# Encoder step on one core: the first three weight units as one operand of 328 columns

## The chip, the cores and the metric

The kernel runs on one core of one Trainium2 chip. The metric is the device time in microseconds (us) of one execution. The kernel before took 838.03, 839.92 and 839.5 us in three runs, median 839.5 us.

## What is computed

Two layers of a streaming encoder over 320 tokens (256 of a prompt, 64 of a running stream), width 1024. Each layer projects, attends in two branches, and adds two normalised sublayers:

```
h = x @ w_in
A = band attention (8 heads, learned bias by distance)
B = sparse attention (8 heads, rotary); an indexer picks the keys:
    score[t,s] = sum_h w[t,h] * relu(q_idx[t,h] . k_idx[s])
x = LayerNorm(alpha * x + concat(A, B) @ w_out)
x = LayerNorm(alpha * x + relu(x @ w_up)^2 @ w_down)
```

Only the projection of layer 0 and the indexer behind it matter here. The indexer key has 64 columns of `w_in` and the indexer weights 8 more (together `ki`, 72 columns); the indexer queries are four blocks of 128 columns (`qi0` to `qi3`).

## The kernel before

Weights come in **units** of 1024 x 128 (8 row blocks of 128 rows). Layer 0 begins with the units ki (unit 0, 72 columns), qi0, qi3, qi2, qi1 (units 1 to 4), then qa0, qa1, va2, ka0, va1, ka1 and so on (units 5 to 10 and up). Two units lie next to each other in HBM and come as one load of 1024 KB (`load_raw`, L151) into one of two buffers named `raw`; a third load waits until the pair two before it is split. So the loads behind the first three units are the pairs (3,4), (5,6), (7,8), (9,10), (11,12), (13,14).

All products are float32 made of three: a unit is **split** into a rounded high part `wh` (ScalarE, L170) and the rest `wl` (VectorE, L176), and so is x; `mm3` (L188 to L190) then multiplies hi*hi, hi*lo and lo*hi into the same bank. A unit takes 8 x 3 = 24 matmuls of 320 columns. `project` multiplies one unit with all 8 row blocks of x and hands the bank to the unit's use. Four PSUM banks are for these products (`main_acc`), four (`at`) for everything else, so a set of three `at` banks must be emptied before the next set but one can begin.

The uses of the first units, in words:

- ki: ScalarE evacuates the bank (L284), doubles the 64 rows (L492) and swaps halves (`swap`, L292, four instructions); VectorE rotates (`rotate`, L295 to L297), and the finished key is written out (`o_ki`, L499, a DMA on SP).
- qi0 to qi3: evacuate, swap, rotate in the same way. Then a **round of dots** (`Index.dots`, L533 and L535) multiplies the query with the keys into three `at` banks, `clip` (L541, ScalarE, three instructions) empties them, and `weigh` adds them up. After four rounds VectorE begins to pick keys.

No engine chooses its order at run time. The program is written down in the order of a virtual clock: every use is put on an agenda (`later`) with a delay from the table `WAIT`, each `mm3` advances the clock by `NEXT`, and what is due is written into the queues of the engines. `prefetch(i + AHEAD)`, called when a projection begins, writes the splits of the next four units ahead of that. Each queue (ScalarE, VectorE, TensorE, GpSimd and SP, which issues all DMAs) then runs strictly in that order. SP also waits, before each DMA, for the landing of the eighth DMA before it. In SP's queue the write of `o_ki` stands ahead of the bias loads of the first band pair (`u<-rel`, six loads, L341), two cache loads (`kca`, `vca`), and the load of units 11 and 12; then follow the same loads for the next two pairs and the load of units 13 and 14.

At the start, x comes in five loads, ki and qi0 by two row blocks at a time, qi3 in two halves; units 0 and 1 are multiplied together, row block by row block, and unit 2 after them. The split parts of the first three units take three of the five `wh`/`wl` buffers, and units 1 and 2 take one of the two `raw` buffers.

Of the kernel before, what the change touches and what calls it, by code (L numbers as in the profile page):

```python
# [11 lines left out]
F32 = mybir.dt.float32  # L12
F32R = mybir.dt.float32r
AF = mybir.ActivationFunctionType
ALU = mybir.AluOpType

P = 128
DEPTH = 2
D = 1024
KD = D // P  # L20
TP = 256
TS = 64
T = TP + TS
TX = T + 2
# [10 lines left out]
TAKEN = -3.0e38  # L35
BARRED = -1.0e38
N_UNIT = 67
N_DIST = 447
AHEAD = 4
N_DEFER = 7  # L40
N_OUTER = 2
N_SIDE = 4
N_WARM = 7
N_TAIL = 4
TOKENS = slice(0, P), slice(P, 2 * P), slice(T - P, T)
WAIT = [{"lo": 3.4, "rope": 4.6, "scores": 3.4, "peaks": 0.0, "exps": 1.0, "normalise": 5.6, "turn": 3.0,
# [18 lines left out]
NEXT = 3 * 0.136  # L65
# [4 lines left out]
def encoder_step(ctx: ExitStack, tc: tile.TileContext, a: dict):  # L70
    nc = tc.nc
# [11 lines left out]
    def st(shape, tag, bufs, dt=F32):  # L83
        uid[0] += 1
        return sb.tile(shape, dt, name=f"{tag}_{uid[0]}", tag=tag, bufs=bufs)
# [22 lines left out]
    def unit(dt=F32, w=T):  # L108
        return st([P, 3 * P], "u", N_UNIT, dt)[:, :w]

# [28 lines left out]
    raw = {}  # L139
    split = {}  # L140
    at = {"raw": 0, "split": 0}

    def load_raw(i):
        l, c = units[i]
        if c is None:
            t = st([P, 2, KD, P], "raw", 2)
            nc.sync.dma_start(t[:, 0, :, :72], a["w_ki"][l])
            raw[i] = t[:, 0, :, :72]
        elif c % 2 == 0:
            t = st([P, 2, KD, P], "raw", 2)  # L150
            nc.sync.dma_start(t, a["w_all"][l, c // 2])  # L151
            raw[i] = t[:, 0]
            raw[i + 1] = t[:, 1]

    def need_raw(upto):
        while at["raw"] <= min(upto, len(units) - 1):
            load_raw(at["raw"])
            at["raw"] += 1
# [22 lines left out]
    def until(ready):  # L181
        while not ready():
            advance(NEXT)
# [9 lines left out]
    x = ct([P, KD, T], "x")  # L193
# [3 lines left out]
    rope = ct([P, 4, T], "rope")  # L197
    ln = ct([P, DEPTH, 4, KD], "ln")
# [1 line left out]

    nc.gpsimd.memset(mean_w, -1.0 / D)
    xs = [(unit(F32R), unit(F32R)) for _ in range(KD)]
    pair0 = st([P, 2, KD, P], "raw", 2)
    raw[0], raw[1], raw[2] = st([P, KD, TX], "rl", 1)[:, :, :72], pair0[:, 0], pair0[:, 1]
    ins = a["w_ki"][0], a["w_all"][0, 0, :, 0], a["w_all"][0, 0, :, 1]
    for i, n in enumerate((72, P, P)):
        split[i] = [st([P, KD, P], t, 5, F32R)[:, :, :n] for t in ("wh", "wl")]
    at["raw"], at["split"] = 3, 3
    cuts = [slice(0, 1), slice(1, 2)] + [slice(k, k + 2) for k in range(2, KD, 2)]
    for g in cuts:  # L210
        nc.sync.dma_start(x[:, g], a["xT"][:, g])
        if g.start != 1:
            g = slice(g.start - g.start % 2, g.start + 2)
            for i in range(2):
                nc.sync.dma_start(raw[i][:, g], ins[i][:, g])
    for g in (slice(0, 4), slice(4, KD)):
        nc.sync.dma_start(raw[2][:, g], ins[2][:, g])
    need_raw(3)
    make_identity(nc, ident)
    nc.gpsimd.memset(eps, EPS)  # L220
    warm = main_acc()
    for _ in range(N_WARM):
        nc.tensor.matmul(warm[:, :P], mean_w, mean_w, start=True, stop=True)

    def split_rows(i, g):
        hi, lo = split[i]
        nc.scalar.activation(hi[:, g], raw[i][:, g], AF.Copy)  # L227
        nc.vector.tensor_tensor(lo[:, g], raw[i][:, g], hi[:, g].bitcast(F32), op=ALU.subtract)  # L228

    for g in cuts:  # L230
        for k in range(g.start, g.stop):
            nc.scalar.activation(xs[k][0], x[:, k], AF.Copy)
            nc.vector.tensor_tensor(xs[k][1], x[:, k], xs[k][0].bitcast(F32), op=ALU.subtract)  # L233
        if g.start != 1:
            g = slice(g.start - g.start % 2, g.start + 2)
            for i in range(2):
                split_rows(i, g)
    for g in (slice(0, 4), slice(4, KD)):
        split_rows(2, g)
    need_raw(5)  # L240
    nc.sync.dma_start(rope, a["rope"])
    nc.sync.dma_start(ln, a["ln"])
    fresh = set(range(KD))
    whole = {0, 1, 2}
    rh, rl = st([P, KD, TX], "rh", 1, F32R), st([P, KD, TX], "rl", 1, F32R)

    stats = []

    def project(i, defer, *uses):

        prefetch(i + len(uses) - 1 + AHEAD)
        accs = []
        for n in range(len(uses)):
            accs.append(main_acc()[:split[i + n][0].shape[2]])
        for k in range(KD):
            until(lambda: k in (norm.ready if defer else fresh))
            for n, p in enumerate(accs):
                if defer:
                    mm3(p[:, :TX], i + n, k, rh[:, k], rl[:, k], k == 0, k == KD - 1)
                else:  # L260
                    mm3(p[:, :T], i + n, k, *xs[k], k == 0, k == KD - 1)

        def settle(p, use):
            if not stats:
                later(NEXT, settle, p, use)
                return
            n = p.shape[0]
            mu, rstd = stats
            c, u = st([P, 1], "c", 6)[:n], temp("z", 3)[:n]
            nc.vector.scalar_tensor_tensor(u, mu[:n], p[:, T:T + 1], p[:, :T], op0=ALU.mult, op1=ALU.add)  # L270
            nc.vector.tensor_copy(c, p[:, T + 1:TX])
            nc.vector.tensor_tensor(u, u, rstd[:n], op=ALU.mult)  # L272
            later(NEXT, use, (u, c))

        for p, use in zip(accs, uses):
            if defer:
                settle(p, use)
            else:
                use((p[:, :T], None))
# [383 lines left out]
    class LastNorm(Norm):  # L663


        def __init__(self, l, which):
            super().__init__(l, which, False)
            self.rg = st([P, KD, TX], "rh", 1)[:, :, :T]
            self.g_row = st([P, KD, TX], "rl", 1)[0:1, 0:4].rearrange("p k t -> p (k t)")[:, :D]
            nc.sync.dma_start(self.g_row, a["g_last"])  # L670
            self.ones = unit(w=P)
            nc.gpsimd.memset(self.ones, 1.0)
# [76 lines left out]
    for l in range(DEPTH):  # L749
# [25 lines left out]
        for s, (name, j) in enumerate(W_IN_ORDER[l]):  # L775
            br = name[1]
            if name[1] in "ab" and (br, j) not in pairs:
                pairs[br, j] = Pair(l, br, j, bias_tiles(l, j) if br == "a" else index.mask)
            uses.append(partial(take, name, j))
            if l > 0 or s > 0:  # L780
                project(base + s + 1 - len(uses), l > 0 and s < N_DEFER, *uses)
                uses = []

# [5 lines left out]
        accs = [main_acc() for _ in range(N_OUTER)]  # L789
# [5 lines left out]
        for m in range(KD):  # L795
            if m < N_OUTER:
                p = accs[m]
            else:
                prefetch(wo + m + AHEAD)
                p = main_acc()  # L800
# [26 lines left out]
        for m in range(KD):  # L827
            if m % 2 == 0:
                later(2.0, before.apply, m)
            p = main_acc()  # L830
# [10 lines left out]
        if not final:  # L841
            fresh.clear()
            xs = [(unit(F32R), unit(F32R)) for _ in range(KD)]
# [24 lines left out]
def lay_out(i):  # L868
    c = np.ascontiguousarray
    xt = np.concatenate([i["x_prompt"][0], i["x_sample"][0]], 0)  # L870
    out = {"xT": c(xt.T.reshape(KD, P, T).transpose(1, 0, 2)), "rope": rope_tables()}
    w = i["w_in"].reshape(DEPTH, KD, P, -1)
    out["w_ki"] = c(w[:, :, :, KI_AT:KI_AT + 72].transpose(0, 2, 1, 3))

    def blocks(w, starts):
        b = np.stack([w[:, :, :, s:s + P] for s in starts], 1)
        return b.transpose(0, 1, 3, 2, 4)

    starts = [[W_IN_AT[n] + P * j for n, j in order if n != "ki"] for order in W_IN_ORDER]
    parts = [np.concatenate([blocks(w[l:l + 1], starts[l]) for l in range(DEPTH)])]  # L880
    parts.append(blocks(i["w_out"].reshape(DEPTH, KD, P, D), range(0, D, P)))
    parts.append(blocks(i["w_up"].reshape(DEPTH, KD, P, DFF), range(0, DFF, P)))
    wd = i["w_down"].reshape(DEPTH, 4, KD, P, KD, P).transpose(0, 4, 1, 3, 2, 5)
    parts.append(wd.reshape(DEPTH, 32, P, KD, P))
    wa = np.concatenate(parts, 1)
    out["w_all"] = c(wa.reshape(DEPTH, 50, 2, P, KD, P).transpose(0, 1, 3, 2, 4, 5))
    for br in "ab":
        k = i[f"cache_{br}_k"][:, 0]
        out["kc" + br] = c(k.reshape(DEPTH, PAST, NPAIR, P).transpose(0, 2, 3, 1))
        v = i[f"cache_{br}_v"][:, 0]  # L890
        out["vc" + br] = c(v.reshape(DEPTH, 2, P, NPAIR, P).transpose(0, 3, 2, 1, 4))
    ki = i["cache_b_kidx"][:, 0].transpose(0, 2, 1)
    out["kidx"] = c(np.concatenate([ki, ki], 1))
    r = i["rel_bias"]
    out["rel"] = c(np.concatenate([np.repeat(r[:, :, 256:], N_DIST - 256, 2), r[:, :, :0:-1]], 2))
    lns = np.stack([i["ln1_g"], i["ln1_b"], i["ln2_g"], i["ln2_b"]], 1)
    out["g_last"] = c(i["ln2_g"][DEPTH - 1:])
    out["ln"] = c(lns.reshape(DEPTH, 4, KD, P).transpose(3, 0, 1, 2))
    return out
# [33 lines left out]
```

## Time and profile before

| | before |
|---|---|
| median of three runs | 839.5 us (838.03 to 839.92) |
| profiled execution | 836.99 us, span 835.2 us |
| mean granted clock of TensorE | 0.993 of full |
| TensorE matmul busy | 821.1 us, 98% of the span |
| VectorE, ScalarE busy | 594.6 us (71%), 494.0 us (59%) |
| DMA | 124.05 MB, mean 149 GB/s |

The span is what the profile covers; the execution's own time is 1.8 us longer. Busy shares are means over the whole kernel, and the change touches the first stage only, so the rows further down are those of the first 70 us. An "idle before" in square brackets ends with what released the engine.

### The profile page before, as it was taken

Reading aid. Unit: us, or ns where it says so; the run is one execution under the profiler, and the core shown is the slowest. Engines: PE = TensorE matmul, PEld = TensorE weight load, DVE = VectorE, ACT = ScalarE, POOL = GpSimd, SP = SyncE. Lnnn points to the kernel's source line nnn. Section 1 sums busy time; section 2 is a strip of 40 time slices with the busy share of each in tenths; the row PEclk is TensorE's granted clock in tenths of the full one; section 3 lists DMA queues with packets and bytes.
Section 4 is the critical chain, followed back from the end, with each engine's and each line's share of the span. In section 5 each row is a group of like instructions: output and inputs, shape, how many; then the busy total and the mean of one; then the engine's idle time right before and its main releaser. Section 6 shows DMA issues by size and latency. Waiting matters only on the chain.

```text
span 835.2 us, 15008 instructions
## 1 busy us (share of the span) xinstructions
PE 821.1 (98%) x5792; PEld 794.3 (95%) x5792; DVE 594.6 (71%) x1284; ACT 494.0 (59%) x955; POOL 28.7 (3%) x145
## 2 busy tenths in 40 slices
PE   9979999999999999999998999999999999999997
PEld 7969999999999999999998989999999999999995
DVE  5649878586998883545496679996699888545343
ACT  6846798565665553434358977885556655434332
POOL 0110000000000000000000010110000000000000
PEclk9999999999999999999999999999999999999998
DMA  8676343343444444534687324342334444434411
GB/s 275 192 191 180 135 143 126 125 151 103 151 156 147 152 154 149 177 127 155 194 171 261 108 101 135 120 177 74 136 145 151 152 151 152 160 144 152 151 51 64
DMA packets 35033, 124.05 MB, mean 149 GB/s; under 512 B 6033, under 2 KB 21521, under 8 KB 22290
## 3 DMA queue, kind: packets, MB, share of 16 engines
q1 hardware_dynamic: 34962, 123.10, 44.6%
q8 instruction: 46, 0.75, 0.4%
q14 instruction: 25, 0.20, 0.1%
HBM read 116.36 MB, written 6.72 MB: 147 GB/s over the span
## 4 chain that ended last, share of the span: by engine, by line
PE 75%; DVE 10%; ACT 8%; DMA 4%; SPq 1%; issue 1%; ACTq 0%; DVEq 0%
PE mm L188 23%; PE mm L189 23%; PE mm L190 23%; DMA raw<-w_all 4%; DVE wl L176 2%; ACT u L292 2%; ACT wh L170 2%; ACT u L418 1%; DVE u L577 1%; PE at L442 1%; DVE m L575 1%; PE at L394 1%; DVE u L410 1%; PE at L461 1%; PE at L396 1%
## 5 line engine op out<-in xcount | busy, mean ns | idle before, releaser
L188 PE MATMUL mm<-u,wh 128*128 128x320 f32 (+1 forms) x1048 | 328.8, 314 | 0.3 <-ACT wh L227 0.2
L190 PE MATMUL mm<-u,wl 128*128 128x320 f32 (+1 forms) x1048 | 324.0, 309 | 0.4 <-DVE wl L176 0.3
L189 PE MATMUL mm<-u,wh 128*128 128x320 f32 (+1 forms) x1048 | 323.8, 309 | 0.2 <-DVE u L233 0.2
L170 ACT ACTIVATE wh<-raw 128x1024 fp32r<-128x1024 f32 x199 | 209.5, 1055 | 182.9 <-PE mm L189 108.4
L176 DVE TENSOR_TENSOR wl<-raw,wh 128x1024 fp32r<-128x1024 f32 x199 | 241.3, 1217 | 57.8 <-ACT wh L170 57.3
L188 PEld LDWEIGHTS mm<-u,wh 128*128 128x128 f32 (+1 forms) x1048 | 196.8, 188 | 2.1 <-ACT wh L227 1.0
L190 PEld LDWEIGHTS mm<-u,wl 128*128 128x128 f32 (+1 forms) x1048 | 196.5, 187 | 1.6 <-DVE wl L228 0.9
L189 PEld LDWEIGHTS mm<-u,wh 128*128 128x128 f32 (+1 forms) x1048 | 196.9, 188 | 0.4 <-DVE u L233 0.4
L188 PE MATMUL mm<-rh,wh 128*128 128x322 f32 x568 | 177.5, 313 | 0.0
L190 PE MATMUL mm<-rh,wl 128*128 128x322 f32 x568 | 176.2, 310 | 0.0
L189 PE MATMUL mm<-rl,wh 128*128 128x322 f32 x568 | 175.8, 310 | 0.0
L189 PEld LDWEIGHTS mm<-rl,wh 128*128 128x128 f32 x568 | 107.2, 189 | 0.2
L188 PEld LDWEIGHTS mm<-rh,wh 128*128 128x128 f32 x568 | 107.1, 189 | 0.2
L190 PEld LDWEIGHTS mm<-rh,wl 128*128 128x128 f32 x568 | 106.5, 188 | 0.0
L603 DVE SCALAR_TENSOR_TENSOR x<-x,mm 128x320 f32<-128x320 f32 x31 | 15.0, 487 | 78.9 <-PE mm L190 78.9
L292 ACT ACTIVATE u<-u 32x320 f32<-32x320 f32 x104 | 48.7, 469 | 1.8
L270 DVE SCALAR_TENSOR_TENSOR z<-mu,mm 128x320 f32<-128x320 f32 x71 | 38.7, 545 | 12.7 <-PE mm L190 12.7
L811 ACT ACTIVATE z<-z,c 128x320 f32<-128x320 f32 x64 | 35.8, 560 | 16.8 <-DVE z L272 15.8
L418 ACT ACTIVATE u<-u,mx 128x128 f32<-128x128 f32 (+2 forms) x80 | 37.0, 464 | 8.9 <-DVE mx L413 8.9
L605 ACT ACTIVATE rh<-x,ln 128x320 fp32r<-128x320 f32 x24 | 13.5, 563 | 45.4 <-DVE x L603 45.4
L818 DVE TENSOR_TENSOR u<-h,u 128x320 fp32r<-128x320 f32 x64 | 31.5, 492 | 7.2 <-DVE h L817 0.5
L272 DVE TENSOR_TENSOR z<-z,rstd 128x320 f32<-128x320 f32 x71 | 34.9, 492 | 0.0
(135 smaller groups left out, 710.4 us busy)
## 6 DMA issues: line engine op xcount, KB each, us to landing
raw<-w_all SPq DMA_DIRECT2D x99, 1024.0 KB, 4.8
u<-rel SPq DMA_DIRECT2D x16, 128.0 KB, 5.5
u<-rel SPq DMA_DIRECT2D x16, 80.0 KB, 5.8
o_va<-u SPq DMA_DIRECT2D x8, 160.0 KB, 5.3
o_ka<-u SPq DMA_DIRECT2D x8, 160.0 KB, 2.3
o_kb<-u SPq DMA_DIRECT2D x8, 160.0 KB, 1.8
o_vb<-u SPq DMA_DIRECT2D x8, 160.0 KB, 1.8
o_y<-x SPq DMA_DIRECT2D x8, 160.0 KB, 1.9
```

What stands on the lines that cost most here:

```text
L170: nc.scalar.activation(hi, w, AF.Copy)
L176: nc.vector.tensor_tensor(lo, w, hi.bitcast(F32), op=ALU.subtract)
L188: nc.tensor.matmul(out, hi[:, k], xh, start=first, stop=False)
L189: nc.tensor.matmul(out, hi[:, k], xl, start=False, stop=False)
L190: nc.tensor.matmul(out, lo[:, k], xh, start=False, stop=last)
L270: nc.vector.scalar_tensor_tensor(u, mu[:n], p[:, T:T + 1], p[:, :T], op0=ALU.mult, op1=ALU.add)
L272: nc.vector.tensor_tensor(u, u, rstd[:n], op=ALU.mult)
L292: nc.scalar.activation(dst[32 * q:32 * q + 32], src[32 * (q ^ 1):32 * (q ^ 1) + 32], AF.Copy)
L418: nc.scalar.activation(p, p, AF.Exp, bias=self.mx[:, i:i + 1], scale=1.0, accum_out=self.sums[:, i:i + 1])
L603: nc.vector.scalar_tensor_tensor(r, r, ALPHA, psum, op0=ALU.mult, op1=ALU.add)
L811: nc.scalar.activation(u, u, AF.Relu, bias=b)
L818: nc.vector.tensor_tensor(hl, h, hh.bitcast(F32), op=ALU.subtract)
```

## The change

The first three units become one operand of 328 columns (72 + 128 + 128), laid out on the host as `w_first`, row block by row block. It comes in eight loads of 164 KB, one per row block, into general buffers; the first two are issued by ScalarE, the rest by SP between the loads of x. Each row block is split as a whole into the buffers `rh`/`rl`, that are free at this time, so all five `wh`/`wl` buffers and both `raw` buffers stay free. The three units are multiplied in one call of `project`: per row block nine matmuls. The load of units 3 and 4 is cut in two halves. There is one warming matmul less.

```
-N_WARM = 7
+N_FIRST = 3
+FIRST_W = 72 + 2 * P
+N_WARM = 6
...
+            if i == N_FIRST:
+                for n in range(2):
+                    nc.sync.dma_start(t[:, n], a["w_all"][l, c // 2, :, n])
+            else:
+                nc.sync.dma_start(t, a["w_all"][l, c // 2])
...
+    fw = [unit(w=FIRST_W) for _ in range(KD)]
+    fh, fl = st([P, KD, FIRST_W], "rh", 1, F32R), st([P, KD, FIRST_W], "rl", 1, F32R)
+    for i, (c0, c1) in enumerate(((0, 72), (72, 72 + P), (72 + P, FIRST_W))):
+        split[i] = fh[:, :, c0:c1], fl[:, :, c0:c1]
...
+    for k in range(2):
+        nc.scalar.dma_start(fw[k], a["w_first"][:, k])
     for g in cuts:
         nc.sync.dma_start(x[:, g], a["xT"][:, g])
+        for k in range(max(g.start, 2), g.stop):
+            nc.sync.dma_start(fw[k], a["w_first"][:, k])
     need_raw(3)
+    nc.sync.dma_start(rope, a["rope"])
+    need_raw(5)
+    nc.sync.dma_start(ln, a["ln"])
...
+    for k in range(KD):
+        nc.scalar.activation(xs[k][0], x[:, k], AF.Copy)
+        if k == 0:
+            nc.vector.tensor_copy(fh[:, k], fw[k])
+        else:
+            nc.scalar.activation(fh[:, k], fw[k], AF.Copy)
+        nc.vector.tensor_tensor(xs[k][1], x[:, k], xs[k][0].bitcast(F32), op=ALU.subtract)
+        nc.vector.tensor_tensor(fl[:, k], fw[k], fh[:, k].bitcast(F32), op=ALU.subtract)
...
+            if i == 0:
+                for part, of in ((0, 0), (0, 1), (1, 0)):
+                    for n, p in enumerate(accs):
+                        nc.tensor.matmul(p[:, :T], split[n][part][:, k], xs[k][of], start=k == 0 and part + of == 0,
+                                         stop=k == KD - 1 and part == 1)
+                advance(N_FIRST * NEXT)
+                continue
...
-            if l > 0 or s > 0:
+            if l > 0 or s > N_FIRST - 2:
                 project(base + s + 1 - len(uses), l > 0 and s < N_DEFER, *uses)
```

Because `project` now begins with three units, its first call of `prefetch` writes the splits of units 3 to 6 (before: 3 to 5), and the uses of ki, qi0 and qi3 are all due after the same projection. That moves instructions in the queues. Behind the third round of dots, the queues of TensorE, ScalarE and VectorE stand as before.

On VectorE, where the indexer key is rotated (before: `u_325` is the key, `u_169` is qi0, `wl_257` unit 6). Before:

```order
L176 TENSOR_TENSOR wl_182<-raw_163,wh_181 128x1024 [waits DMAHW0_49,PE_49,Activation_49]
L176 TENSOR_TENSOR wl_257<-raw_163,wh_256 128x1024 [waits PE_49,Activation_49]
L295 TENSOR_TENSOR u_169<-u_249,rope 128x320 [waits DMAHW1_49]
L296 TENSOR_TENSOR u_250<-u_250,rope 128x320
L297 TENSOR_TENSOR u_169<-u_169,u_250 128x320 [waits DVE_49]
L295 TENSOR_TENSOR u_325<-u_240,rope 128x320
L296 TENSOR_TENSOR u_241<-u_241,rope 128x320
L297 TENSOR_TENSOR u_325<-u_325,u_241 128x320 [waits DVE_49]
```

Now (`u_363` is the key, `u_165` qi0, `u_168` qi3, `wl_291` unit 7):

```order
L182 TENSOR_TENSOR wl_181<-raw_116,wh_180 128x1024 [waits Activation_49]
L182 TENSOR_TENSOR wl_291<-raw_215,wh_290 128x1024 [waits DMAHW3_49,Activation_49]
L297 TENSOR_TENSOR u_165<-u_276,rope 128x320 [waits DMAHW7_49]
L298 TENSOR_TENSOR u_277<-u_277,rope 128x320
L299 TENSOR_TENSOR u_165<-u_165,u_277 128x320 [waits DVE_49]
L297 TENSOR_TENSOR u_168<-u_283,rope 128x320
L298 TENSOR_TENSOR u_284<-u_284,rope 128x320
L299 TENSOR_TENSOR u_168<-u_168,u_284 128x320 [waits DVE_49]
L297 TENSOR_TENSOR u_363<-u_267,rope 128x320
L298 TENSOR_TENSOR u_268<-u_268,rope 128x320
L299 TENSOR_TENSOR u_363<-u_363,u_268 128x320 [waits DVE_49]
```

The rotation of the key stood behind the split of unit 6 and the rotation of qi0; now it stands behind the split of unit 7 and the rotations of qi0 and qi3. ScalarE's half of the split of unit 7 (`wh_290`) stands in its queue behind the evacuation and swap of qi3.

On ScalarE, where the first rounds of dots are emptied (before: `u_519` to `u_521` first round, `u_597` on second round, `wh_557` unit 11). Before:

```order
L170 ACTIVATE wh_475<-raw_299 128x1024 [waits DVE_49]
L541 ACTIVATE u_519<-at_510 128x384 [waits PE_49]
L541 ACTIVATE u_520<-at_511 128x384 [waits PE_49]
L541 ACTIVATE u_521<-at_512 128x320 [waits PE_49]
L284 ACTIVATE u_465<-mm_478 128x320 [waits PE_49]
L170 ACTIVATE wh_557<-raw_422 128x1024 [waits DMAHW7_49,DVE_49]
L541 ACTIVATE u_597<-at_588 128x384 [waits PE_49]
```

Now (`u_573` to `u_575` first round, `u_596` on second round, `wh_533` unit 11):

```order
L176 ACTIVATE wh_471<-raw_219 128x1024 [waits DVE_49]
L286 ACTIVATE u_461<-mm_474 128x320 [waits PE_49]
L176 ACTIVATE wh_533<-raw_418 128x1024 [waits DMAHW6_49,DVE_49]
L543 ACTIVATE u_573<-at_564 128x384 [waits PE_49]
L543 ACTIVATE u_574<-at_565 128x384 [waits PE_49]
L543 ACTIVATE u_575<-at_566 128x320 [waits PE_49]
L543 ACTIVATE u_596<-at_587 128x384 [waits PE_49]
```

The split of unit 11 stood behind the first round's clip; now it stands ahead of it.

On TensorE, the rounds of dots themselves. Before, the first round stood among the matmuls of unit 6 and the second among those of unit 7. Now both stand at the end of unit 7 (`mm_536`):

```order
L537 MATMUL at_566<-u_363,u_165 128x64
L194 MATMUL mm_536<-u_87,wh_290 128x320
L195 MATMUL mm_536<-u_88,wh_290 128x320
L196 MATMUL mm_536<-u_87,wl_291 128x320
L535 MATMUL at_587<-u_363,u_168 128x128 [waits DVE_49]
L535 MATMUL at_588<-u_363,u_168 128x128 [waits Activation_49]
```

The second round follows the first after three matmuls, and its second bank (`at_588`) is one that the first round's clip empties.

## Rows read from the trace of the kernel before

**Rows 1.** The page, part 1: busy us, share of the span, instructions.

```profile
PE 821.1 (98%) x5792; PEld 794.3 (95%) x5792; DVE 594.6 (71%) x1284; ACT 494.0 (59%) x955; POOL 28.7 (3%) x145
```

**Rows 2.** TensorE's waits, 0 to 70 us: total us, times, longest us.

```profile
PE at L394 <- ACT u L328: 2.6, 1, 2.6
PE at L533 <- ACT u L541: 1.7, 1, 1.7
```

**Rows 3.** ScalarE's timeline: start us, us, operation, count, idle before.

```profile
18.46 1.07 ACT L170 ACTIVATE wh<-raw 128x1024 fp32r<-128x1024 f32 x1 [0.92 <-DMA raw<-w_all]
...
26.16 0.42 ACT L284 ACTIVATE u<-mm 128x320 f32<-128x320 f32 x1
...
28.55 1.06 ACT L170 ACTIVATE wh<-raw 128x1024 fp32r<-128x1024 f32 x1
29.52 0.42 ACT L284 ACTIVATE u<-mm 128x320 f32<-128x320 f32 x1
...
43.98 1.06 ACT L170 ACTIVATE wh<-raw 128x1024 fp32r<-128x1024 f32 x1 [4.97 <-DMA raw<-w_all]
```

**Rows 4.** ScalarE's timeline at the load of units 13 and 14.

```profile
57.42 1.06 ACT L170 ACTIVATE wh<-raw 128x1024 fp32r<-128x1024 f32 x1 [8.61 <-DMA raw<-w_all]
58.65 0.26 ACT L328 ACTIVATE u<-at 64x128 f32<-64x128 f32 x1
```

**Rows 5.** SP's timeline: the write of `o_ki`, the load of units 11 and 12.

```profile
30.25 0.56 SPq L499 DMA_DIRECT2D o_ki<-u  x1
...
35.95 0.37 SPq L151 DMA_DIRECT2D raw<-w_all  x1
```

**Rows 6.** TensorE's timeline: first and last matmul of unit 2.

```profile
13.64 0.31 PE L188 MATMUL mm<-u,wh 128*128 128x320 f32 x1
...
17.02 0.31 PE L190 MATMUL mm<-u,wl 128*128 128x320 f32 x1
```

**Rows 7.** Stretches: us, busy us by engine (PE, PEld, DVE, ACT, POOL), PEclk, DMA share, GB/s.

```profile
2.00:4.00 2.00, 2.00 (x11) 2.00 (x10) 0.38 (x1) 0.77 (x3) 0.00 (x0) 1.00 0.71 196
2.00:12.00 10.00, 9.41 (x48) 7.25 (x48) 5.98 (x16) 6.33 (x18) 0.00 (x0) 1.00 0.89 278
16.00:20.00 4.00, 3.72 (x26) 3.46 (x25) 2.81 (x3) 3.05 (x5) 0.00 (x0) 1.00 1.04 401
31.00:32.00 1.00, 1.00 (x8) 1.00 (x8) 1.00 (x3) 0.96 (x3) 0.00 (x0) 1.00 0.79 303
32.00:34.00 2.00, 2.00 (x17) 1.42 (x15) 1.73 (x3) 1.96 (x4) 0.53 (x3) 1.00 0.54 62
60.00:65.00 5.00, 5.00 (x19) 4.17 (x17) 5.00 (x18) 3.70 (x6) 0.00 (x0) 0.50 0.15 53
```

**Rows 8.** VectorE's timeline: the key's rotation begins, and what follows it.

```profile
28.76 0.48 DVE L295 TENSOR_TENSOR u<-u,rope 128x320 f32<-128x320 f32 x1
...
30.14 0.17 DVE L514 TENSOR_SCALAR wi<-at 128x20 f32<-128x20 f32 x1
```

**Rows 9.** TensorE's timeline, rounds of dots, and the band scores of L394.

```profile
37.62 1.33 PE L533 MATMUL at<-u,u 64*128 64x128 f32 x8
43.24 0.48 PE L533 MATMUL at<-u,u 64*128 64x128 f32 x2
45.47 0.92 PE L533 MATMUL at<-u,u 64*128 64x128 f32 x6 [1.74 <-ACT u L541]
58.96 2.02 PE L394 MATMUL at<-u,u 64*128 64x128 f32 x8 [2.65 <-ACT u L328]
```

**Rows 10.** TensorE's timeline at the two levels of the clock.

```profile
62.62 0.47 PE L189 MATMUL mm<-u,wh 128*128 128x320 f32 x1
...
65.29 0.47 PE L190 MATMUL mm<-u,wl 128*128 128x320 f32 x1
...
71.38 0.93 PE L394 MATMUL at<-u,u 64*128 64x128 f32 x8
...
73.14 0.31 PE L189 MATMUL mm<-u,wh 128*128 128x320 f32 x1
```

More of the change, by code (lines that the diff above doesn't have):

```diff
@@ L150, in load_raw @@
             t = st([P, 2, KD, P], "raw", 2)
-            nc.sync.dma_start(t, a["w_all"][l, c // 2])
+            if i == N_FIRST:
[3 more added lines that the diff above has]
+                nc.sync.dma_start(t, a["w_all"][l, c // 2])
             raw[i] = t[:, 0]
@@ L202, in encoder_step @@
     xs = [(unit(F32R), unit(F32R)) for _ in range(KD)]
[L203 to L208, printed above, removed]
+    fw = [unit(w=FIRST_W) for _ in range(KD)]
+    fh, fl = st([P, KD, FIRST_W], "rh", 1, F32R), st([P, KD, FIRST_W], "rl", 1, F32R)
+    for i, (c0, c1) in enumerate(((0, 72), (72, 72 + P), (72 + P, FIRST_W))):
+        split[i] = fh[:, :, c0:c1], fl[:, :, c0:c1]
+    at["raw"], at["split"] = N_FIRST, N_FIRST
+    whole = set(range(N_FIRST))
     cuts = [slice(0, 1), slice(1, 2)] + [slice(k, k + 2) for k in range(2, KD, 2)]
+    for k in range(2):
+        nc.scalar.dma_start(fw[k], a["w_first"][:, k])
     for g in cuts:
         nc.sync.dma_start(x[:, g], a["xT"][:, g])
[L212 to L217, printed above, removed]
+        for k in range(max(g.start, 2), g.stop):
+            nc.sync.dma_start(fw[k], a["w_first"][:, k])
     need_raw(3)
+    nc.sync.dma_start(rope, a["rope"])
+    need_raw(5)
+    nc.sync.dma_start(ln, a["ln"])
     make_identity(nc, ident)
@@ L223, in encoder_step @@
         nc.tensor.matmul(warm[:, :P], mean_w, mean_w, start=True, stop=True)
[L225 to L242, printed above, removed]
+    for k in range(KD):
[6 more added lines that the diff above has]
+        nc.vector.tensor_tensor(fl[:, k], fw[k], fh[:, k].bitcast(F32), op=ALU.subtract)
     fresh = set(range(KD))
-    whole = {0, 1, 2}
-    rh, rl = st([P, KD, TX], "rh", 1, F32R), st([P, KD, TX], "rl", 1, F32R)
+    rh, rl = [st([P, KD, FIRST_W], t, 1, F32R)[:, :, :TX] for t in ("rh", "rl")]
     stats = []
@@ L667, in __init__ @@
             super().__init__(l, which, False)
-            self.rg = st([P, KD, TX], "rh", 1)[:, :, :T]
-            self.g_row = st([P, KD, TX], "rl", 1)[0:1, 0:4].rearrange("p k t -> p (k t)")[:, :D]
+            self.rg = st([P, KD, FIRST_W], "rh", 1)[:, :, :T]
+            self.g_row = st([P, KD, FIRST_W], "rl", 1)[0:1, 0:4].rearrange("p k t -> p (k t)")[:, :D]
             nc.sync.dma_start(self.g_row, a["g_last"])
@@ L886, in lay_out @@
     out["w_all"] = c(wa.reshape(DEPTH, 50, 2, P, KD, P).transpose(0, 1, 3, 2, 4, 5))
+    out["w_first"] = c(np.concatenate([out["w_ki"][0], out["w_all"][0, 0, :, 0], out["w_all"][0, 0, :, 1]], 2))
     for br in "ab":
```

## The prediction

> **What bounds the kernel now.** The page comes first: TensorE is busy for 98% of the span [rows 1], so all that can be lost or won is in the few places where it waits or runs at its lower clock. The profiled execution took 836.99 us (span 835.2 and 1.8 around it), 2.5 below the median of the three runs, 839.5; the sum is made against 836.99 and its difference is then laid on the median. The list of TensorE's waits up to 70 us comes next [rows 2]: two that are not small, 2.6 us before band scores (L394) and 1.7 us before a round of dots (L533). The timelines say what ends them. Both times the releaser is a ScalarE instruction that is itself stuck in ScalarE's queue behind the split of a unit whose load has not landed: at 43.98 the split of unit 11 after 4.97 us of idle time [rows 3], at 57.42 that of unit 13 after 8.61 [rows 4]. So in the first 60 us the kernel is bound by when loads are issued and land, and TensorE's queue only shows it. What starts these loads is in SP's queue: the load of units 11 and 12 is issued at 35.95, behind the bias loads, and these behind the write of the indexer key at 30.25 [rows 5]. The reader should see a chain: a key is rotated on VectorE, SP writes it, the bias loads follow, then unit 11 lands, ScalarE moves on, TensorE moves on.
>
> **The change, step by step.** The front itself: the 72 matmuls of the first three units stay 72, of about 0.147 us each (23 steps from 13.64 to 17.02 [rows 6]); their last begins at 17.02 now and would begin some 2 us earlier if weights arrive evenly. The smaller edits (one warming matmul, two loads issued by ScalarE ahead of its table load, one copy on VectorE, a strided weight) I cost at nothing: they lie in these 17 us, and a wait of some 12 us, derived below, covers whatever the front gains or loses. If that cover is gone, the front is worth its 2 us.
>
> *Step 1, when units 5 and 6 land.* They now need no buffer of unit 1 and are issued early, but everything before them must be moved: 1280 KB of x, 1312 of first weights, 1024 of units 3 and 4, 640 of rope, 1024 of their own (from the shapes), 5280 KB or 5.41 MB. The first 2.65 MB at the 278 GB/s of 2 to 12 [rows 7] from 2.0 us on take 9.5 us, the other 2.75 MB at 401 (16 to 20 [rows 7]) 6.9: 18.4. The engines were only 0.71 busy at 196 GB/s in 2 to 4 [rows 7], where now two queues issue; I take 0.5 off: 17.9. Before, ScalarE began unit 5 at 18.46, just after it landed [rows 3]. Term: -0.5. Bounds: 401 GB/s from the start gives 15.5 (-2.9); 240 GB/s for the first part gives 20 (+1.5).
>
> In the trace, transfers of 72 to 320 KB, up to eight at a time, moved 278 GB/s together [rows 7]. The Trainium skill, DMA: Bandwidth & Descriptors, section Rules for kernel authors with the table of section Bandwidth, speaks against this edit: batch to 1 MiB (341 GB/s), since 64 KB gets 138. An estimate between these entries for 164 KB is 207 GB/s; the first part would take 12.8 us and the sum below would be 3.3 higher. The trace does not agree; I keep the row.
>
> *Step 2, from unit 5 to the write of the key.* Before: 18.46 to 30.25. ScalarE and VectorE run this stretch without a break from one piece to the next, so pieces add. New ahead of the key's rotation are: qi3's evacuation and swap, from 26.16 to 28.55 [rows 3], 2.39; ScalarE's split of unit 7, 28.55 to 29.52 [rows 3], 0.97; and qi3's rotation, for which the key's own from 28.76 to 30.14 [rows 8] stands, 1.38. VectorE's split of unit 7 takes the place of unit 6's. Term: +4.74. The write goes out at 30.25 - 0.5 + 4.74 = 34.5.
>
> *Step 3, from that write to the split of unit 11.* SP's queue holds the same eight loads in between, so 13.73 us as from 30.25 to 43.98 [rows 3, 5]. What was left of units 9 and 10 (303 GB/s in 31 to 32, against 62 after [rows 7]) has now landed earlier, since their buffer is free by 21; these 0.3 MB are worth 0 (the engines idle half the time in 32 to 34) to 1.5 us. I take -0.5. Unit 11's split begins at 47.7.
>
> *Step 4, the new wait.* On ScalarE that split now stands ahead of the first round's clip, on TensorE the second round needs the first round's banks, and all of TensorE's queue is behind it. Before, the clip behind the split was the second round's, and TensorE stopped in the third round: it resumed at 45.47 [rows 9], 1.49 after the split began. Now it stops in the second round, by 37 or so: unit 4 needs ki's bank, evacuated at about 17.9 + 2.0 + 0.4 = 20.3, and then follow four units of 3.5 and some 2.4 of dots. It resumes at 47.7 + 1.49 = 49.2, after a wait of 12 us. From the second round's stop to the third's it still has the work of 37.62 to 43.24 [rows 9] less three matmuls, 5.62 - 0.44 = 5.18. So it stands at the third round at 54.4, where before it went on at 45.47: +8.9.
>
> *Step 5, the wait that goes.* Units 13 and 14 hang on the same chain and land 3.74 later: the instruction of L328 that ends the old wait comes at 58.9 + 3.7 = 62.6 [rows 4]. TensorE arrives there at 58.96 - 2.65 + 8.9 = 65.2 [rows 9], so the 2.65 us fall away: +8.9 - 2.65 = **+6.3**. What is late next is TensorE itself, and no wait follows up to 70 that could take it back [rows 2].
>
> *Step 6, the clock.* After the 2.65 us of idle time the granted clock stood at 0.50, 1.2 GHz in 60 to 65 [rows 7]. It cost 58.96 to 62.62 against 71.38 to 73.14 for the same instructions, 1.9, and ten steps from 62.62 to 65.29 at 0.267 instead of 0.147 [rows 10], 1.2: 3.1 us. After the change that stretch is gone, and one follows the wait of 12 us; I take the same 3.1, term 0. Bounds: half as long, -1.6; a second stretch, +3.1.
>
> The sum is -0.5 + 4.74 - 0.5 + 5.18 - 2.65 = +6.3: 843.3 for a profiled execution, **845.8** on the median.
>
> **The rivals.** (a) *The front's gain reaches the end*: the three units are done 2 us earlier and nothing behind gives it back, 837.5. It needs the second round not to wait, that is, unit 11 landed by 36; the load would have to be issued by 28 and the key written by 22, and step 2 puts that write at 32 at the earliest. Only another order than the one shown could do that. (b) *It cancels*: units 5 and 6 land at 15.5, the bias loads gain 1.5 and the clock recovers in half the time: 6.3 - 2.4 - 1.0 - 1.6 = +1.3, 840.8. For it speaks that the engines carry 401 GB/s with large rows; against it that all three must come together. (c) *Slower still, by the clock*: TensorE falls to 1.2 GHz twice, after the new wait and again when units 13 or 15 are short: +9.4, 848.9. For it: it fell after a wait of only 2.65 us. (d) *Slow first loads*: were the first 2.65 MB moved at the 196 GB/s of 2 to 4 us throughout, they would take 13.5 us instead of 9.5, +4.0: 849.8; the row of 2 to 12 is against it. By the Trainium skill's rule cited in step 1 it would be 849.1. That the three units are not multiplied together is no rival, the order shows it.
>
> **The numbers.** The forecast gets 0.67; (a) 0.05; (b) 0.08; (c) 0.15; (d) 0.05. One measurement can tell about 0.2% from no change, 1.7 us here. (a) is faster, (b) lies within 1.7, the rest is slower: 0.05, 0.08, 0.87. The forecast's own range is its bounds of steps 1 to 3 without the rarest ends, +3 to +8.5; with (c) and (d), and the upper part between it and (b), 841.5 to 849.5.
>
> **What would show it.** Right: the write of the key near 34.5, with DMA engines idle for several us before it; unit 11's split near 47.7; TensorE's longest wait at the second round of dots, 8 to 13 us, released by ScalarE's clip; no wait before L394; a stretch at 0.50 of clock right after 49. Step 1 is checked by the first split of unit 5 (17.9). Wrong, if the second round of dots goes through without a long wait, or if TensorE reaches the scores of L394 before 61.

## The result, and the profile after

The changed kernel took 843.67 us (median of 7 runs, 841.67 to 846.41), the kernel before beside it 838.03 (7 runs, 835.40 to 841.21): ratio 1.007, 95% interval 1.0041 to 1.0099. It is slower by 5.6 us, where 6.3 were forecast. The forecast of 845.8 is 2.1 us high, and 1.5 of that is its base: more runs of the kernel before brought its median from 839.5 down to 838.0. The profiled execution took 843.67 us with a span of 841.6, 6.4 over the span of before.

TensorE's two longest waits in the first 70 us of the changed kernel (total us, times, longest), where before two stood of 2.6 and 1.7 [rows 2]:

```profile
PE at L535 <- ACT u L543: 12.4, 1, 12.4
PE mm L194 <- ACT u L286: 1.0, 1, 1.0
```

Both old waits are gone and one of 12.4 us stands at the second round of dots. ScalarE's timeline says what it waits for (start us, us, operation, count, idle before and its end); its lines answer to [rows 3, 4]:

```profile
17.60 2.00 ACT L176 ACTIVATE wh<-raw 128x1024 fp32r<-128x1024 f32 x2 [3.08 <-DMA raw<-w_all]
...
48.34 1.06 ACT L176 ACTIVATE wh<-raw 128x1024 fp32r<-128x1024 f32 x1 [11.29 <-DMA raw<-w_all]
49.30 1.18 ACT L543 ACTIVATE u<-at 128x384 f32<-128x384 f32 x3
...
62.50 1.06 ACT L176 ACTIVATE wh<-raw 128x1024 fp32r<-128x1024 f32 x1 [2.79 <-DMA raw<-w_all]
```

The clip at 49.30 is what TensorE needs; it stands in ScalarE's queue behind the split of unit 11, and that split sat 11.29 us for its load. Why the load is late is in SP's timeline, which answers to [rows 5]:

```profile
34.11 0.55 SPq L501 DMA_DIRECT2D o_ki<-u  x1
34.71 4.35 SPq L343 DMA_DIRECT2D u<-rel  x6
...
40.26 0.37 SPq L157 DMA_DIRECT2D raw<-w_all  x1
```

The key's write has moved from 30.25 to 34.11, and behind it the load of units 11 and 12 from 35.95 to 40.26. How the transfers of these microseconds lie is seen in the stretches (columns as in [rows 7]):

```profile
2.00:12.00 10.00, 9.35 (x59) 8.86 (x59) 7.15 (x17) 7.11 (x16) 0.00 (x0) 1.00 1.01 350
12.00:14.00 2.00, 2.00 (x16) 1.98 (x15) 0.74 (x1) 1.60 (x2) 0.00 (x0) 1.00 1.05 436
14.00:16.00 2.00, 2.00 (x16) 1.99 (x15) 1.71 (x2) 0.52 (x1) 0.00 (x0) 1.00 1.01 423
...
28.00:32.00 4.00, 4.00 (x29) 4.00 (x28) 3.18 (x6) 3.91 (x7) 0.45 (x2) 1.00 0.00 0
...
40.00:44.00 4.00, 0.00 (x0) 0.00 (x0) 0.24 (x1) 0.00 (x0) 0.67 (x5) 0.68 0.99 137
44.00:49.80 5.80, 0.00 (x0) 0.00 (x0) 0.00 (x0) 1.46 (x3) 0.84 (x7) 0.50 0.95 317
49.80:55.00 5.20, 5.17 (x19) 4.34 (x20) 4.60 (x11) 3.31 (x7) 1.71 (x9) 0.50 0.86 85
55.00:60.00 5.00, 5.00 (x36) 4.42 (x36) 1.50 (x5) 1.68 (x4) 1.07 (x6) 0.99 0.90 283
```

Read the last column and the one before it. From 28 to 32 us nothing moves at all: everything that may be loaded is loaded, and SP stands before the key's write. Twelve microseconds later the engines are full (0.99), at only 137 GB/s, because the bias loads go ahead of the weights. The column PEclk shows the price on TensorE: while it waits the granted clock falls to 0.50, 1.2 GHz, and the work from 49.8 to 55 runs at it.

TensorE's own timeline, which answers to [rows 9]:

```profile
36.91 0.48 PE L535 MATMUL at<-u,u 64*128 64x128 f32 x2
49.83 1.65 PE L535 MATMUL at<-u,u 64*128 64x128 f32 x6 [12.44 <-ACT u L543]
...
57.02 0.93 PE L535 MATMUL at<-u,u 64*128 64x128 f32 x8
...
67.79 0.93 PE L396 MATMUL at<-u,u 64*128 64x128 f32 x8
...
72.05 0.49 PE L328 MATMUL at<-ident,u 128*128 128x128 f32 x3
...
455.00 0.93 PE L396 MATMUL at<-u,u 64*128 64x128 f32 x8 [2.37 <-ACT u L290]
```

and in the kernel before the same transposes, which come after its second wait and its own half-clock stretch, and the same wait of the second layer:

```profile
66.55 0.49 PE L326 MATMUL at<-ident,u 128*128 128x128 f32 x3
...
449.42 0.93 PE L394 MATMUL at<-u,u 64*128 64x128 f32 x8 [2.39 <-ACT u L288]
```

At the band scores (L396, before L394) the changed kernel is 67.79 - 58.96 = 8.8 us late; by the transposes it has won 3.3 back, since before ran that stretch at half clock, and is 72.05 - 66.55 = 5.5 late. These 5.5 stay: in the second layer a wait that both kernels have ends at 449.42 before and at 455.00 after, 5.6 apart. So nearly all that the change costs is lost ahead of 72 us. The last 0.8 of the 6.4 between the two spans is lost behind 826 us: the matmuls of L733 (L735 after) begin 5.8 apart, at 825.77 and 831.57, and take 0.78 us before and 1.35 after. Whether the change has a part in that is not shown.

### The profile page after: what moved, and what is told of

The parts are those of the page before. It is cut to its first block, busy times and chain, and to the rows that moved or that the text cites. A ratio compares the mean times of both kernels' runs of the same rounds, so it can differ in the third digit from the quotient of the medians.

```text
span 841.6 us, 14987 instructions
## 1 busy us (share of the span) xinstructions
PE 819.6 (97%) x5790; PEld 793.7 (94%) x5790; DVE 594.7 (71%) x1283; ACT 493.6 (59%) x952; POOL 28.8 (3%) x145
## 4 chain that ended last, share of the span: by engine, by line
PE 84%; DVE 7%; ACT 4%; DMA 4%; issue 1%; ACTq 0%; DVEq 0%
PE mm L194 25%; PE mm L196 25%; PE mm L195 25%; DMA raw<-w_all 3%; DVE wl L182 2%; PE at L444 2%; PE at L463 1%; ACT wh L176 1%; PE at L396 1%; DVE u L579 1%; PE at L398 1%; ACT u L294 1%; DVE m L577 1%; PE at L535 1%; DMA u<-w_first 1%; DVE x L647 1%
## 5 line engine op out<-in xcount | busy, mean ns | idle before, releaser
L194 PE MATMUL mm<-u,wh 128*128 128x320 f32 x1024 | 321.4, 314 | 1.0 <-ACT u L286 1.0
L195 PE MATMUL mm<-u,wh 128*128 128x320 f32 x1024 | 316.8, 309 | 0.0
L196 PE MATMUL mm<-u,wl 128*128 128x320 f32 x1024 | 316.8, 309 | 0.0
L194 PEld LDWEIGHTS mm<-u,wh 128*128 128x128 f32 x1024 | 192.5, 188 | 2.0 <-ACT u L286 1.3
L195 PEld LDWEIGHTS mm<-u,wh 128*128 128x128 f32 x1024 | 192.5, 188 | 0.0
L196 PEld LDWEIGHTS mm<-u,wl 128*128 128x128 f32 x1024 | 192.3, 188 | 0.0
```

The source lines that it names most:

```text
L194: nc.tensor.matmul(out, hi[:, k], xh, start=first, stop=False)
L195: nc.tensor.matmul(out, hi[:, k], xl, start=False, stop=False)
L196: nc.tensor.matmul(out, lo[:, k], xh, start=False, stop=last)
```

## The experiments

Two questions: what of the loss is SP's queue, and what would be left of the new front without it. Below, the ratio is always to the kernel before on the same chip, whose median was 837.5 us beside all runs but the last three and 839.2 beside those.

**The key's write put later.** `later` queues the write in SP's order behind the load of units 13 and 14. The same edit was made in the changed kernel and in the kernel before.

```diff
-            nc.sync.dma_start(a["o_ki"][self.l], self.k[0:64])
+            later(12.0 if self.l == 0 else 0.0, nc.sync.dma_start, a["o_ki"][self.l], self.k[0:64])
```

In the changed kernel:

> The changed kernel; only the write of the indexer key is put into SP's queue later (behind the load of units 13 and 14) instead of ahead of the first bias loads. Theory 1 (the time is lost in the queues: the key's write holds up the loads behind it, and unit 11's split holds up the first clip): SP goes on to the bias loads at about 21.5 us, the load of units 11 and 12 then waits only for the split of unit 8 and is issued at about 35.3 instead of 40.3, and lands at 40.5 to 43; TensorE's wait at the second round of dots ends at 42 to 44.5 instead of 49.8. 5 to 7.5 us less than the changed kernel, so 836 to 839 us, a ratio to before of 0.997 to 1.001. Theory 2 (the new front itself costs the time: first weights in slices, two queues, the different splits): no difference, ratio 1.006 to 1.008.

Measured 837.84 us (12 runs), ratio 1.0004 (0.9989 to 1.0019): with one line moved the changed kernel is level with the kernel before. SP and then ScalarE of this kernel, and its longest wait on TensorE:

```profile
35.95 0.33 SPq L157 DMA_DIRECT2D raw<-w_all  x1
...
47.90 0.75 SPq L130 DMA_DIRECT2D o_ki<-u  x1
```

```profile
40.80 1.06 ACT L176 ACTIVATE wh<-raw 128x1024 fp32r<-128x1024 f32 x1 [3.14 <-DMA raw<-w_all]
```

```profile
PE at L535 <- ACT u L543: 4.3, 1, 4.3
```

The first six bias loads now go out before 26 us, ahead of the stretch in which nothing moved, the weight load goes 4.3 us earlier and needs 4.9 us to its split instead of 8.1, as no bias loads lie ahead of it. TensorE's wait shrinks from 12.4 to 4.3 us. In the kernel before:

> The kernel before, with the write of ki's key put in SP's queue later, as in key_late. SP stood from about 27.9 to 30.25 us for that write, with the load of units 11 and 12 behind it. T1 (the whole loss of the change is that one queue: the order of the three units costs nothing once no load stands behind the key's write): before and after come out alike when neither has it, so this kernel is within 0.2% of key_late, a ratio to the kernel before of 0.998 to 1.001. T2 (the key that comes 4.7 us later also delays other things than the load, by a path that key_late left in): this kernel gains the 1.74 us wait ahead of the dots and its half-clock stretch on top, a ratio of 0.994 to 0.997, clearly below key_late's 1.0004.

Measured 835.65 (11 runs), ratio 0.9977 (0.9964 to 0.9990). So before paid for this write too, some 2 us: its wait of 1.7 us at the dots [rows 2] is down to 0.3.

```profile
PE at L533 <- ACT u L541: 0.3, 1, 0.3
```

This lies between the two theories: the edited kernels are 0.27% apart (give or take 0.2), more than T1 allowed, less than T2 asked for. So the write in SP's queue accounts for some 0.4 of the 0.7% that the change lost. The rest fits the 4.3 us wait left in the changed kernel; the run with both edits, below, bears on that.

**The split behind the clips.** In the changed kernel alone, the split of unit 11 is moved on ScalarE behind the first clips.

```diff
-        prefetch(i + len(uses) - 1 + AHEAD)
+        prefetch(i + len(uses) - 1 + AHEAD - (i == 7))
```

> The changed kernel; only the prefetch at unit 7 reaches one unit less far, so that the split of unit 11 stands behind the clips of the first two rounds of dots on ScalarE. The key's write stays where it is. Theory 1: the wait of 12 us at the second round goes, the second and third round pass, the fourth waits 2 to 3 us for unit 11 (landing at 48.3 as before), but the load of units 13 and 14 still lands at about 62.4, so TensorE now waits some 7 us before the band scores (until about 63.9 instead of arriving at 67.8): 3.5 to 4.5 us less than the changed kernel, 839 to 840.5 us, ratio 1.002 to 1.004. Theory 2: ratio 1.006 to 1.008.

Measured 841.77 (5 runs), ratio 1.0047 (1.0035 to 1.0059), a quarter of a per cent won against the changed kernel's 1.007, and less than T1 asked for (1.002 to 1.004). Its longest waits on TensorE up to 80 us:

```profile
PE at L396 <- ACT u L330: 7.4, 1, 7.4
PE at L537 <- POOL u L355: 1.5, 1, 1.5
PE at L535 <- ACT u L543: 1.4, 1, 1.4
```

The wait of 12.4 us is now 10.3 in three pieces, the largest at the band scores, for the next late load. Order on ScalarE mainly says where TensorE stops; how long is said by the load. With the load early as well, the two edits together:

> The changed kernel with both edits: the key's write late in SP's queue, and ScalarE's split of unit 11 behind the clips of the first dots' rounds. key_late has one wait of 4.3 us at the second round of dots and 5 us at half clock behind it; its unit 13 is split at 55.0 us and TensorE comes to the dots of pair a at 60.4. T1 (the wait is the clip standing behind the split, and what it costs is wait plus half clock): the 4.3 us and some 2.5 us of pace go, TensorE comes to the dots of pair a at 53 to 54 and waits there about 3 us for the clip behind unit 13's split; net 3 to 4 us under key_late, a ratio to the kernel before of 0.995 to 0.998. T2 (the next load, which has not moved, sets the time anyway, as the 7.4 us wait in clip_first did): the wait only moves, 0.999 to 1.002.

Measured 833.97 (10 runs), ratio 0.9968 (0.9948 to 0.9988). That is under the late write alone (1.0004) and level with the kernel before with its write late (0.9977): without the 4.3 us wait nothing of the loss is left. One wait of more than a microsecond is left up to 80 us, for the load of units 13 and 14, as T1 had it (3 us):

```profile
PE at L396 <- ACT u L330: 3.0, 1, 3.0
```

**Two units together, then the third.** The new operand, its loads and its front stay, but units 0 and 1 are multiplied together and unit 2 behind them, as in the kernel before.

```diff
-            if l > 0 or s > N_FIRST - 2:
+            if l > 0 or s > 0:
```

(and, in `project`, `split[i + n]` and `advance(len(uses) * NEXT)` for the two groups.)

> The changed kernel with all of its new loads and splits of the first three units; only the multiplication is as before: ki and qi0 together, row block by row block, and qi3 after them, so that uses and splits behind it stand in the old order on all engines. Theory 1: the key is written at about 29.4 us (before: 30.25, changed: 34.1), since units 5 and 6 land 0.9 us earlier than before; all of the chain behind it is earlier by about that: 0 to 1.5 us less than the kernel before, ratio 0.998 to 1.000. Theory 2: the front still has its cost, ratio 1.004 or more.

Measured 839.06 (12 runs), ratio 1.0011 (0.9996 to 1.0027). It misses T1's range (0.998 to 1.000) by little, and T2's (1.004 or more) clearly: the loss is the three-at-once order; the loads and the operand cost 0.3% at most. Its key is written at 30.16, as early as before:

```profile
30.16 0.57 SPq L501 DMA_DIRECT2D o_ki<-u  x1
```

and the gain that T1 hoped for from the front isn't there either: unit 5's split starts at 18.39 in this run, before at 18.46 [rows 3]. The key hangs on that load, not on the first matmuls, so their being done earlier buys nothing here. The two waits of before are there in other sizes (4.1 us at the dots, before 1.7; 0.9 at the band scores, before 2.6), since the load of units 11 and 12, issued at 35.25, needed 10.2 us to its split at 45.42; why longer than the 8.0 of before is not shown.

```profile
PE at L535 <- ACT u L543: 4.1, 2, 3.3
...
PE at L396 <- ACT u L330: 0.9, 1, 0.9
```

**The clock during the wait.** 84 matmuls of 320 columns whose result nothing reads are put ahead of the second round of dots, to keep TensorE at work while it waits.

```diff
+            if self.l == 0 and j == 3:
+                idle = main_acc()
+                for _ in range(N_FILL):
+                    nc.tensor.matmul(idle[:, :T], split[8][0][:, 0], xs[0][0], start=True, stop=True)
```

> The changed kernel; 84 matmuls of 320 columns that nothing reads are put into TensorE's queue ahead of the second round of dots, so that it works (84 x 0.147 = 12.3 us) through most of the 12.4 us in which it waited. It computes the same. What the wait costs beside its length, by the clock: if the granted clock now stays at full speed behind 49.8 us, the 5.2 us at half speed (49.8 to 55.0) go back to about 2.6: 1.5 to 2.6 us less than the changed kernel, 841 to 842.2 us, ratio 1.0035 to 1.005. If the clock is no part of the loss: the same as the changed kernel, ratio 1.006 to 1.008.

Measured 842.89 (6 runs), ratio 1.0055 (1.0038 to 1.0072), between the two expectations, which by itself decides nothing. The trace does; first TensorE's timeline with the filling, then the stretches:

```profile
39.62 12.48 PE L537 MATMUL mm<-u,wh 128*128 128x320 f32 x84
52.03 0.93 PE L540 MATMUL at<-u,u 64*128 64x128 f32 x8
...
71.85 0.49 PE L329 MATMUL at<-ident,u 128*128 128x128 f32 x3
```

```profile
44.00:49.80 5.80, 5.80 (x42) 5.80 (x41) 0.00 (x0) 0.00 (x0) 0.76 (x5) 1.00 1.02 315
49.80:55.00 5.20, 5.20 (x38) 4.62 (x37) 3.64 (x9) 4.16 (x9) 2.40 (x12) 1.00 0.82 111
```

The granted clock stays at full speed where it was 0.50. The dots begin at 52.03, and the transposes of L328 (here L329) come at 71.85, 19.8 us later; without the filling it is 72.05 - 49.83 = 22.2 from the end of the wait. So the half-clock stretch costs some 2.4 us. In this execution unit 11 is split at 49.82, so the clip would have set TensorE free at 51.3 (49.82 + 1.49, as in the run without it), and the filling holds it 0.7 longer: this crude filling gives back 1.7. The total of this execution, 845.0 us, can't be set beside this, since it has another half-clock stretch, that the changed kernel has not: behind unit 5's split, here only at 18.89, TensorE waits 1.9 us where the changed kernel waits 1.0, and the granted clock is 0.58 from 22 to 26 us.

**The second chain.** In the kernel before, the load of units 13 and 14 stands in SP's queue behind the bias loads of band pair 2, which is taken up after pairs 0 and 1. The edit puts these bias loads off.

```diff
-                pairs[br, j] = Pair(l, br, j, bias_tiles(l, j) if br == "a" else index.mask)
+                late = br == "a" and l == 0 and j == 2
+                pairs[br, j] = Pair(l, br, j, None if late else bias_tiles(l, j) if br == "a" else index.mask)
+            if l == 0 and (name, j) == ("ka", 2):
+                pairs[br, j].add = bias_tiles(l, j)
```

> The kernel before, with the eight bias, kca and vca loads of band pair 2 issued a projection later, behind the load of units 13 and 14 instead of ahead of it. T1 (the wait of 2.65 us at the dots of band pair 1 and the 3 us of work at half clock behind it come from that weight load's place in SP's queue): both go, 3 to 4 us less, a ratio of 0.995 to 0.997, and the next load takes over at most part of it. T2 (the transfer's start isn't set by the bias loads but by the buffer of raw, or the bias tiles are then late at pair 2): 0.999 to 1.003, with a wait of the same size there or at pair 2.

Measured 842.01 (7 runs), ratio 1.0065 (1.0041 to 1.0088): slower. SP and TensorE:

```profile
78.85 3.36 SPq L341 DMA_DIRECT2D u<-rel  x6
```

```profile
58.44 0.93 PE L394 MATMUL at<-u,u 64*128 64x128 f32 x8
...
67.52 0.93 PE L394 MATMUL at<-u,u 64*128 64x128 f32 x8
...
90.02 1.54 PE L396 MATMUL at<-u,u 128*128 128x256 f32 x4 [6.34 <-POOL u L353]
```

T1's first half holds: the wait of 2.65 us at L394 is gone, and this kernel reaches the second band scores at 67.52, before at 71.38 [rows 10]. But the deferred loads stood in SP's queue behind writes of `o_va` and `o_ka` that wait for compute, went out at 78.85, and TensorE waited 6.3 us for GpSimd, which finishes their tiles. The same loss, made the same way, a stage later. The kernel with two units then one, the late key's write and the same deferral does it too:

> The front of the changed kernel with its operand of 328 columns, but units 0 and 1 multiplied together and unit 2 behind them as in the kernel before, with the key's write late and the loads of band pair 2 deferred. T1 (the two waits of the first 70 us and their half-clock stretches are set by the places of two weight loads in SP's queue): neither wait is left, 4 to 7 us under the kernel before, a ratio of 0.991 to 0.996. T2 (with one wait gone the next one stands in its place, since the loads of the first 70 us take as long as the work): 0.997 to 1.001.

Measured 836.70 (12 runs), ratio 0.9998 (0.9979 to 1.0016). It has no wait of a microsecond from 2 to 78 us and reaches the second band scores at 63.01, where before does at 71.38 [rows 10]; then come 6.2 us of waiting and a stretch at half clock. T2's number, but by a wait for the deferred bias loads, not for the next weights:

```profile
85.70 1.54 PE L398 MATMUL at<-u,u 128*128 128x256 f32 x4 [6.24 <-POOL u L355]
```

**All three put right.** The deferred loads go out between the two writes of `o_va`, where SP would stand anyway (`s == 12` in place of the test on `ka`), together with the late write of the key: in the kernel before, in the changed kernel (with the split behind the clips), and in the one with two units, then one.

> The kernel before with the key's write late in SP's queue, and the six rel loads of band pair 2 two steps earlier than in pair2_before: between the two writes of va, while SP stands for the second of them from 67.5 to 73.9 us. In pair2_before they went out at 78.85 and TensorE waited 6.3 us at pair 2 for GpSimd, which fills their corners. T1 (a weight load's place in the queue sets both early waits, and the rel loads of pair 2 have slack between 51 and some 80 us): neither the 2.65 us wait at pair 1 nor the 6.3 us at pair 2 is there, no half-clock stretch before 80 us, 4 to 8 us under the kernel before, a ratio of 0.990 to 0.995. T2 (the rel loads find no free place in the first 80 us): a wait of 2 us or more at pair 3, pair 2 or the next split, a ratio of 0.997 to 1.004.

Measured 830.61 (6 runs), ratio 0.9908 (0.9880 to 0.9937).

> The changed kernel with the key's write late, the split of unit 11 behind the clips, and the rel loads of pair 2 between the two writes of va. T1 (the three units at once cost nothing once no weight load stands behind a wait in SP's queue): the 3.0 us wait that key_clip has at pair 1 goes with its half clock, 4 to 8 us under the kernel before, a ratio of 0.990 to 0.995 and within 0.2% of both_before. T2 (three at once, with the first key 4.7 us later, has a price of its own on TensorE): over 0.3% behind both_before.

Measured 832.27 (6 runs), ratio 0.9920 (0.9894 to 0.9946).

> The front of the changed kernel, units 0 and 1 together and unit 2 behind them, with the key's write late and the rel loads of pair 2 between the two writes of va. best1 was without a wait until 78 us and 8 us ahead of the kernel before there, and lost it at pair 2's rel loads (6.2 us, then half clock). T1: that wait is gone, 5 to 9 us under the kernel before, a ratio of 0.989 to 0.994. T2 (the front that ends its 72 matmuls 1.9 us earlier is worth that much once nothing else waits): 0.2% ahead of both_before. T3 (a load of weights is late all the same, the next one in line): 0.997 to 1.002.

Measured 831.31 (6 runs), ratio 0.9908 (0.9877 to 0.9939). All three beat both kernels, by 0.8 to 0.9% against before. The stretch from 40 to 70 us, of the edited kernel before and then of the edited changed kernel:

```profile
40.00:50.00 10.00, 10.00 (x72) 8.89 (x70) 7.55 (x15) 4.83 (x10) 4.08 (x15) 1.00 0.81 233
50.00:60.00 10.00, 10.00 (x69) 9.36 (x70) 5.84 (x21) 6.14 (x12) 0.00 (x0) 1.00 0.43 154
60.00:70.00 10.00, 10.00 (x72) 9.42 (x71) 9.90 (x45) 4.39 (x15) 0.73 (x5) 1.00 0.93 209
```

```profile
40.00:50.00 10.00, 10.00 (x72) 8.84 (x71) 7.47 (x18) 3.41 (x6) 3.56 (x15) 1.00 0.88 237
50.00:60.00 10.00, 10.00 (x69) 9.30 (x68) 6.80 (x27) 6.16 (x12) 0.00 (x0) 1.00 0.46 158
60.00:70.00 10.00, 10.00 (x72) 9.42 (x71) 9.90 (x38) 5.34 (x18) 0.72 (x5) 1.00 0.96 215
```

TensorE is busy throughout at full clock in both. With these waits out of the way, three at once, two then one, and the front of before can't be told apart: the intervals overlap almost wholly, and each is about 2.5 us wide to either side. The three units as one operand are then neither a loss nor a gain that these runs can show; a gain of the 2 us that the prediction gave the front would not be seen.

## Why the prediction was right

The sign, the mechanism and nearly the size held, and the signs that the prediction named came: the write at 34.11 behind some 8 us of idle DMA engines, the long wait at the second round released by the clip, none before the band scores, the half-clock stretch. The terms did less well than their sum, and that the sum came within a microsecond is in part luck.

- **Step 1**, -0.5 for unit 5's load: measured 17.60 against 18.46, -0.9. Near in the end, by luck, and wrong inside: the loads moved at 350 GB/s from 2 to 12 us, not 278, with engines full (1.01), and at 436 and 423 from 12 to 16, above the 401 taken. By these rates the 5.41 MB of the sum would have been in at 16.4. That unit 5 came 1.2 us later is explained only in part: two loads issued behind its own, `ln` and `kidx` (160 KB, some 0.4 us), moved beside it and are not in the sum. The row of before, at 0.89, was no measure of what the new loads carry. The Trainium skill, DMA: Bandwidth & Descriptors, section Rules for kernel authors, asks for 1 MiB or more to a transfer for full bandwidth. The estimate of 207 GB/s that the prediction drew from that page does not fit this row of the changed kernel, in which no load of more than 320 KB had been issued yet and the engines were full (columns as in [rows 7]):

```profile
4.00:6.00 2.00, 1.44 (x9) 1.30 (x10) 1.64 (x5) 1.61 (x4) 0.00 (x0) 1.00 1.05 398
```

  The same first loads put unit 5's split at 17.37 to 18.89 in the nine profiled kernels that have them, so half a microsecond is no finding.
- **Step 2**, +4.74: 34.11 - 17.60 = 16.51 against 11.79, +4.72. The three pieces measured 2.40, 0.97 and 1.37, as taken: adding up what stands in front of a key was exact, on a chain that runs from ScalarE to VectorE without a gap.
- **Step 3**, 13.2 us from the write to unit 11's split: measured 48.34 - 34.11 = 14.2. This term was mis-sized by 1.0. The queues were indeed empty, but the 0.5 taken off didn't come, and another 0.5 came on top. From issue to split the load took 8.1 us as before (8.0). SP needed 6.15 us from the write to the issue, before 5.70: it was longer over the six bias loads, 4.35 us against the 3.26 of this row of before, and 0.6 shorter over the rest:

```profile
30.86 3.26 SPq L341 DMA_DIRECT2D u<-rel  x6
```

- **Step 4**, a wait of 12 us ending at 49.2: 12.44, ending at 49.83, which is 1.49 after the split began, as taken from before.
- **Step 5**, the old wait falls away and TensorE arrives at 65.2: no wait, but 67.79. Of the 2.6 missing, 0.6 came with the end of the wait (step 3's 1.0 less the 0.4 that step 1 was early) and 2.0 are the half clock: the work of 5.18 us up to the third round took 57.02 - 49.83 = 7.19. The step priced this work at full clock and left the clock to step 6.
- **Step 6**, 3.1 us lost at half clock both before and after: 2.4 after, by the filling run, and 3.3 given back between L396 and the transposes. It cancels to within a microsecond, as assumed; that the two stretches come out so near was taken over from before and not derived.

Rival (a) fell: the second round did wait. Whether the front's gain would reach the end where nothing waits stays open, since the last three runs could not show 2 us. (b) fell: unit 5 landed at 17.6 and not 15.5, and the stretch at half clock cost 2.4 us, more than half of the 3.1. (c) fell: one stretch at half clock, not two. (d) fell with step 1. Two readings go beyond the forecast, which named the chain but priced no other order of SP's queue: that moving one line of SP's order brings the changed kernel back level with the kernel before, and that the bias loads, not only the key's write, make each weight load late.

## What to carry to other kernels

Before moving work ahead of a small result, look at who writes that result out, and what stands behind the write in the same queue: here a write of 80 KB that nothing in the kernel waited for held back a weight load, and moving that one write brought the changed kernel from a ratio of 1.007 to 1.0004, and the kernel before to 0.9977. A write that waits for compute belongs behind the loads that don't. Taking away one wait shows nothing until the next one is looked up: the edits of one place each gave 1.0004, 1.0047, 0.9977 and 1.0065, the places put right together 0.991 to 0.992.

## What the runs showed that was not expected

Bias loads fill the DMA engines without moving much, and weights behind them pay. The view of the DMA engines of the changed kernel from 34 to 50 us, in 40 slices (busy tenths, then GB/s):

```profile
DMA  0007211134996969799989899999997999988467
GB/s 0 0 0 175 58 46 38 49 59 87 74 79 93 106 104 170 77 94 95 45 61 79 126 243 378 439 440 410 430 461 299 378 275 227 228 234 273 134 209 246
```

From 38 to 43 us, while the bias loads are on them, the engines are busy for 0.6 to 0.9 and more of a slice and carry 45 to 106 GB/s, in one slice 170; with the weights they carry up to 461. The load of units 11 and 12 took 8.1 us to its split behind bias loads, and 4.9 in the run where they had gone out earlier.

A wait of the same length is not always followed by a lower clock. In the second layer all kernels here but one (3.4 us) have a wait of 2.1 to 2.5 us at the band scores. Behind it the edited kernel before kept its clock, the edited changed kernel did not (the stretch behind the wait, in that order):

```profile
445.00:450.00 5.00, 5.00 (x36) 4.89 (x35) 3.59 (x11) 4.53 (x12) 0.81 (x5) 1.00 0.77 254
```

```profile
445.00:450.00 5.00, 5.00 (x25) 4.28 (x22) 4.96 (x14) 4.13 (x6) 0.81 (x5) 0.66 0.68 210
```

That is 11 fewer matmuls in 5 us, some 1.6 us at 0.147 each, in two programs that differ only in the first 70 us. These two also have a wait each near 80 us, 1.3 and 1.6 us long; behind it, too, the first kept its clock (1.00 from 80 to 85 us) and the second did not (0.66). The profiled executions, 830.71 and 834.06 us, stand 3.4 apart, and such stretches are part of that; it is one reason why the last three kernels are not ranked. What decides whether the clock falls was not tried.
